# A four-layer hybrid decoder trunk: all instructions ordered with the timeline simulation instead of the core simulation

## The chip, the cores and the metric

The kernel runs on one core of one Trainium2 chip. The metric is the device time of one execution in microseconds (us), and the figure that counts is the median of several runs. Engine names in this text: PE (TensorE, matmuls), PEld (its weight loads), DVE (VectorE), ACT (ScalarE), POOL (GpSimd), SP (the queue that issues DMAs).

## The reference

Four layers work on x of 1024 tokens by 1024 channels in float32. Layer i has the token mixer i mod 3, so the order is convolution, S5, RWKV-7, convolution:

```python
for i in range(DEPTH):
    kind, j = i % N_MIXERS, i // N_MIXERS
    ...
    r = DN_ALPHA * x + y
    r = r + (p[i] @ ple_proj[i]) * jax.nn.sigmoid(r @ ple_gate[i])
    x = layer_norm(r, ln_g[i], ln_b[i])
```

Here y is the mixer's result. The convolution mixer is W_out(Bg * conv3(Cg * h) * silu(z)). The S5 mixer is a diagonal complex state-space scan in 64 groups of 16 channels, with a gated linear unit. The RWKV-7 mixer has 16 heads of 64 channels; each head keeps a 64x64 state that is updated token by token with a decay, a delta-rule term and an outer product:

```python
sa = jnp.einsum("bhvk,bhk->bhv", state, -kk_t)
state = (state * w_t[:, :, None, :] + sa[..., None] * (kk_t * a_t)[:, :, None, :]
         + v_t[..., None] * k_t[:, :, None, :])
out = jnp.einsum("bhvk,bhk->bhv", state, r_t)
```

## The kernel before, in words

Channels lie on the 128 partitions, in 8 blocks (`m`), and tokens on the free axis, in two halves of 512 (`h`). Every large product is `mm3` (L308 to L310): operand and weight are each split into a high and a low part, and for each of 8 slices of the inner dimension there are three matmuls of 128x512 (high by high, low by high, high by low), so 24 matmuls for one block and one half, summed in one PSUM bank. The weights come block by block through `wload` (L282 to L286): a DMA of 512 KB from SP's queue, an ACT cast that makes the high part `wh` (L285) and a DVE subtraction that makes the low part `wl` (L286). `wprep` keeps two blocks loaded ahead, from three buffers each.

The RWKV layer does its recurrence in chunks of 64 tokens. For each half it first computes z and v for all blocks, and then goes through the eight blocks in rounds. In a round, for block m:

- the key and the receptance products run (`k_mm` and the `mm3` inside `use_r`; their PSUM tile is `sp`), with the elementwise work on them in `use_k` and `use_r`;
- `prep` forms the chunk matrices (`s`, L1700) and lays their small diagonal blocks side by side with one DVE transpose (L1719, once per round);
- `tsolve` inverts the 16x16 diagonal blocks on DVE, and `join` builds the inverses of the 64x64 chunk matrices from them with 32x32 and 64x64 matmuls (L1780 to L1831);
- `seq` steps through 8 chunks: POOL scales the state (L1856), PE multiplies it (L1857), ACT copies the result (L1858), PE multiplies again (L1861), DVE updates the state (L1864). Then the output is normalised (POOL, L1892) and transposed on PE (L1899).

`join` and `seq` of block m are worked in during the round of block m+1. In the code that reads:

```python
for _ in prio(I.prep(m, h, R), PJ):
    pull(nxt_b)
if m > 0:
    for _ in prio(I.join(m - 1, h, Rs[m - 1]), PJ):
        pass
    inner.append(prio(I.seq(m - 1, h, Rs[m - 1], dVT, dST, dBV, dZ, dY), PS))
tsol.append(prio(I.tsolve(R), PT))
```

The order of the work has two makers. The code traces instructions in a program order, and generators (`pull`) mix background work into it by hand-set counts. That order gives each instruction its priority; `prio` raises the priority of `prep`, `join`, `seq` and `tsolve`. When the `TileContext` closes, a list scheduler goes through the whole trace on a simulated machine: each time an engine of the simulation can take an instruction, it gets the one of highest priority that is ready. What comes out is one fixed sequence of instructions per engine queue, SP's DMA issues among them, and with it the choice of buffers. On the chip each queue then runs in that sequence. A few orders are fixed by hand and hold in any simulation: `issue_after` and `run_of` queue runs of small matmuls behind each other, and `keep_in_program_order` pins the load of the exponential table before the rounds.

The function that opens the context, and that the diff touches:

## Time and profile before

| What | us |
|---|---|
| median of 3 runs | 2887.89 |
| lowest and highest of the runs | 2884.99, 2892.94 |
| the profiled execution, its own time | 2891.85 |
| its span in the profile | 2890.1 |
| PE busy in it | 2732.9 |

The profile is of one execution. Its own time is 1.75 us longer than the span that the trace covers. A busy PE is not PE at its peak: matmuls overlap each other and their weight loads. The granted clock (PEclk, or the column after the engines in a window) is given as a share of full speed. In a line of the chain of waits, "PE p L1861 <- ACT uv L1858: 24.4, 26, 5.4" means that PE stood 24.4 us in all, 26 times, at most 5.4 us, before the instruction of L1861 that writes `p`, until ACT's instruction of L1858 on `uv` was done.

### The profile page before, as it was taken

How to read it: one execution, taken by the hardware profiler on the slowest of the kernel's cores; microseconds unless marked ns; L12 is line 12 of the kernel's file. 1: busy time of each engine (PE TensorE's matmuls, PEld its weight loads, DVE VectorE, ACT ScalarE, POOL GpSimd, SP SyncE). 2: the span in 40 equal slices, each digit the busy share in tenths (PEclk: the TensorE clock that was granted, in tenths of full speed). 3: DMA queues.
4: the chain of work that ended last, by engine and by line, in shares of the span. 5: the costliest groups of instructions: out<-in, count | busy, mean ns of one | idle time of the engine just before them, and what ended most of it. 6: DMA issues, size and time to landing. Idle time of an engine off the chain costs nothing. (4 is left out here: it accounts for less than half of the span.)

```text
span 2890.1 us, 47194 instructions
## 1 busy us (share of the span) xinstructions
PE 2732.9 (95%) x18331; PEld 2164.9 (75%) x18331; DVE 1825.3 (63%) x3396; ACT 1122.2 (39%) x2163; POOL 652.3 (23%) x772
## 2 busy tenths in 40 slices
PE   8999999999999999999887899988899999999998
PEld 6887788778877887676666576766677778888887
DVE  6787855476757348877666587766657473333654
ACT  3333322242254224665455575555434231112322
POOL 1243413121107033102333211333342210000000
PEclk9999999999999999999988799998899999999999
DMA  5333322257873234462222254222334332112321
GB/s 165 97 95 95 95 77 66 88 170 210 224 245 110 88 99 131 155 192 94 78 73 82 77 185 134 85 69 81 102 103 137 104 88 58 52 44 66 117 66 38
DMA packets 449776, 313.10 MB, mean 108 GB/s; under 512 B 48360, under 2 KB 393744, under 8 KB 449552
## 3 DMA queue, kind: packets, MB, share of 16 engines
q1 hardware_dynamic: 449552, 310.08, 35.8%
q8 instruction: 144, 2.36, 0.3%
q14 instruction: 80, 0.66, 0.1%
HBM read 240.28 MB, written 69.21 MB: 107 GB/s over the span
## 5 line engine op out<-in xcount | busy, mean ns | idle before, releaser
L285 ACT CAST wh<-wraw 128x1024 fp32r<-128x1024 f32 x283 | 297.2, 1050 | 699.3 <-PE gp L309 186.5
L286 DVE TENSOR_TENSOR wl<-wraw,wh 128x1024 fp32r<-128x1024 f32 x283 | 369.7, 1306 | 314.9 <-ACT wh L285 309.3
L1856 POOL TENSOR_SCALAR sd<-state,pc 128x128 f32<-128x128 f32 x128 | 94.9, 744 | 214.1 <-DVE state L1864 213.6
L1864 DVE SCALAR_TENSOR_TENSOR state<-p,pc,sd 64x64 f32<-64x64 f32 x256 | 72.2, 282 | 73.6 <-PE p L1861 62.0
L621 POOL TENSOR_TENSOR ln_s<-ln_s,rp 128x512 f32<-128x512 f32 x42 | 61.0, 1452 | 208.1 <-DVE rp L617 208.1
L1861 PE MATMUL p<-uv,kbt 128*128 128x128 f32 x256 | 67.2, 348 | 26.1 <-ACT uv L1858 24.4
L1861 PEld LDWEIGHTS p<-uv,kbt 128*128 128x128 f32 x256 | 44.3, 210 | 57.6 <-ACT uv L1858 49.6
L1857 PE MATMUL p<-state,ra 128*128 128x128 f32 x256 | 64.2, 336 | 15.7 <-DVE state L1864 15.0
L308 PE MATMUL zp<-x_0h,wh 128*128 128x512 f32 x192 | 76.8, 400 | 0.0
L310 PE MATMUL gp<-r_0h,wl 128*128 128x512 f32 x192 | 76.8, 400 | 0.0
L310 PE MATMUL gp<-r_1h,wl 128*128 128x512 f32 x192 | 76.2, 397 | 0.5 <-DVE wl L286 0.5
L1858 ACT COPY uv<-p 64x128 f32<-64x128 f32 x128 | 33.3, 261 | 111.5 <-PE p L1857 109.9
L308 PE MATMUL gp<-r_1h,wh 128*128 128x512 f32 x192 | 76.4, 398 | 0.0
L309 PE MATMUL gp<-r_0l,wh 128*128 128x512 f32 x192 | 76.3, 397 | 0.0
L1857 PEld LDWEIGHTS p<-state,ra 128*128 128x128 f32 x256 | 44.2, 208 | 42.6 <-DVE state L1864 31.2
L308 PE MATMUL gp<-r_0h,wh 128*128 128x512 f32 x192 | 76.1, 396 | 0.0
L308 PE MATMUL zp<-x_1h,wh 128*128 128x512 f32 x192 | 76.0, 396 | 0.0
L310 PE MATMUL zp<-x_0h,wl 128*128 128x512 f32 x192 | 75.8, 395 | 0.0
L310 PE MATMUL zp<-x_1h,wl 128*128 128x512 f32 x192 | 75.7, 395 | 0.0
L309 PE MATMUL zp<-x_1l,wh 128*128 128x512 f32 x192 | 75.7, 394 | 0.0
L309 PE MATMUL zp<-x_0l,wh 128*128 128x512 f32 x192 | 75.7, 394 | 0.0
L636 POOL TENSOR_TENSOR rp<-r_0h,r_0l 128x512 f32<-128x512 f32 x24 | 38.5, 1630 | 164.1 <-PE op L309 164.0
(755 smaller groups left out, 8429.4 us busy)
## 6 DMA issues: line engine op xcount, KB each, us to landing
wraw<-in_conv_w_in_dram SPq DMA_DIRECT2D x80, 512.0 KB
wraw<-in_rwkv_w_rkvz_dram SPq DMA_DIRECT2D x64, 512.0 KB
wraw<-in_ple_gate_dram SPq DMA_DIRECT2D x56, 512.0 KB
wraw<-in_conv_w_out_dram SPq DMA_DIRECT2D x24, 512.0 KB
wraw<-in_ssm_w_in_dram SPq DMA_DIRECT2D x21, 512.0 KB
xt<-xd SPq DMA_DIRECT2D x32, 256.0 KB
wraw<-in_rwkv_w_out_dram SPq DMA_DIRECT2D x16, 512.0 KB
wraw<-in_ple_proj_dram SPq DMA_DIRECT2D x14, 512.0 KB
```

What stands on the lines that cost most here:

```text
L285: nc.scalar.copy(wh, raw)
L286: nc.vector.tensor_tensor(wl, raw, f32(wh[:]), ALU.subtract)
L308: nc.tensor.matmul(ps, lh, xh, start=(k == 0), stop=False)
L309: nc.tensor.matmul(ps, lh, xl, start=False, stop=False)
L310: nc.tensor.matmul(ps, ll, xh, start=False, stop=(k == kt - 1))
L621: nc.gpsimd.tensor_tensor(s, s, rs, ALU.add)
L636: (eng or nc.gpsimd).tensor_tensor(rs, f32(rh[:]), f32(rl[:]), ALU.add)
L1856: G.tensor_scalar(sd, st, R.pc[:, c:c + 1], None, ALU.mult)
L1857: nc.tensor.matmul(p1, R.ra[:, c, :], st, start=False, stop=False, skip_group_check=True)
L1858: SC.copy(uv[rb, :], p1[rb, :])
L1861: last = nc.tensor.matmul(p2[:, 0:P], R.kbt[c // 4][:, c % 4, :], uv, start=True, stop=True)
L1864: V.scalar_tensor_tensor(st[cs, cs], p2[cs, cs], R.pc[cs, c:c + 1], sd[cs, cs], ALU.mult, ALU.add)
```

## The change

One argument is added where the context is opened. The simulated machine on which the scheduler orders the instructions is then the library's timeline simulation instead of its core simulation. The computation, the tiles, the buffers and the dependencies that the code traces are the same.

```diff
-    with tile.TileContext(nc) as tc:
+    with tile.TileContext(nc, schedule_with_timeline_sim=True) as tc:
         body(tc, aps, out)
```

## Prediction

> **What bounds the kernel now.** I read the page first (busy shares and slices), then the windows by stage, then the chain of waits in the one stage that is not full. The page:
>
> ```profile
> span 2890.1 us, 47194 instructions
> PE 2732.9 (95%) x18331; PEld 2164.9 (75%) x18331; DVE 1825.3 (63%) x3396; ACT 1122.2 (39%) x2163; POOL 652.3 (23%) x772
> ...
> PE   8999999999999999999887899988899999999998
> ...
> PEclk9999999999999999999988799998899999999999
> ```
>
> TensorE is busy for 2732.9 of 2890.1 us, so it idles for 157 us; the slices put that idle time, and the low granted clock, mostly into slices 19 to 29. The windows by stage (time, then busy time and count of PE, PEld, DVE, ACT, POOL, then granted clock, DMA share, GB/s) sharpen this:
>
> ```profile
> 0.00:1120.00 1120.00, 1093.90 (x5167) 882.22 (x5168) 726.26 (x1238) 355.44 (x518) 303.27 (x359) 1.00 0.44 127
> 1120.00:1300.00 180.00, 169.13 (x733) 125.47 (x731) 153.19 (x230) 110.57 (x182) 29.84 (x36) 0.98 0.55 174
> 1300.00:1640.00 340.00, 288.22 (x4169) 218.13 (x4169) 233.81 (x579) 177.12 (x464) 102.16 (x139) 0.87 0.26 80
> 1640.00:1800.00 160.00, 145.20 (x743) 110.01 (x741) 113.67 (x196) 101.74 (x204) 24.57 (x25) 0.97 0.49 154
> 1800.00:2120.00 320.00, 282.06 (x4145) 216.32 (x4143) 212.63 (x547) 161.69 (x454) 104.35 (x134) 0.90 0.27 85
> 2330.00:2890.00 560.00, 548.82 (x2457) 448.29 (x2455) 253.81 (x426) 137.74 (x221) 22.62 (x30) 0.99 0.22 65
> ```
>
> Before 1120 us (conv and S5 layers) and after 2330 us (the last conv layer) PE is idle for 26 and 11 us of 1680 us. An order of instructions can give back next to nothing there; it can only lose. The two stretches 1300:1640 and 1800:2120 are the RWKV rounds (per block of 128 channels: key, receptance, `prep`, `tsolve`, `join`, and the recurrence `seq` of the block before). There PE idles for 52 + 38 = 90 us, and the granted clock is 0.87 and 0.90. So these 660 us are where the order decides.
>
> What bounds a round? One instruction marks each: the transpose of L1719, once per round.
>
> ```profile
> 1407.84 1.95 DVE L1719 STREAM_TRANSPOSE mi<-dg 128x1024 f32<-128x1024 f32 x1 [0.34 <-ACT dg L1713]
> 1452.48 1.95 DVE L1719 STREAM_TRANSPOSE mi<-dg 128x1024 f32<-128x1024 f32 x1 [0.34 <-ACT dg L1713]
> ...
> 2011.57 1.95 DVE L1719 STREAM_TRANSPOSE mi<-dg 128x1024 f32<-128x1024 f32 x1 [0.34 <-ACT dg L1713]
> 2054.86 1.95 DVE L1719 STREAM_TRANSPOSE mi<-dg 128x1024 f32<-128x1024 f32 x1 [0.50 <-ACT dg L1713]
> ```
>
> One round took 1452.48 - 1407.84 = 44.6 us, the other 2054.86 - 2011.57 = 43.3 us. Now the wide matmuls (tile sp: the key and receptance products, 128x512) in windows about as long as a round, and the same windows for all work:
>
> ```profile
> 1392.00:1434.00 42.00, 17.22 (x54) 9.36 (x52) 2.79 (x4) 1.24 (x2) 0.96 0.28 88
> ...
> 1519.00:1561.00 42.00, 1.95 (x8) 1.24 (x7) 2.79 (x4) 1.37 (x2) 0.76 0.35 110
> ...
> 2010.00:2050.00 40.00, 0.00 (x0) 0.00 (x0) 2.88 (x4) 0.00 (x0) 0.62 0.13 40
> ```
>
> Around the start of the first of these rounds, 42 us hold 54 wide matmuls among the small ones; the round that began at 2011.57 had none in its first 38 us, and was no shorter. So a round is not set by PE's load: it is a chain through PE, ACT, DVE and POOL of some 43 us, and the wide matmuls ride in its gaps for nothing. That cover is what the order of PE makes.
>
> **The change part by part.** It removes and adds no instruction of the computation, no tile and no buffer. It redraws the order on every queue (PE, ACT, DVE, POOL and the DMA issues of SP) by asking another simulated machine when each instruction is ready. Dependencies, priorities and the orders fixed by hand stay. I can't see the new order; I price it by what an order is worth in each stage.
>
> *Gain: PE instructions that stand too early.* The old order sent some PE instructions out before their input, and the in-order engine stood. From 1120 to 2330 us, PE's waits:
>
> ```profile
> PE p L1861 <- ACT uv L1858: 24.4, 26, 5.4
> PE otp L1899 <- POOL o L1892: 16.4, 14, 2.4
> PE p L1857 <- DVE state L1864: 15.0, 18, 2.2
> ...
> PE ut L1789 <- ACT zi L1786: 10.4, 9, 3.3
> ```
>
> That is 24.4 + 16.4 + 15.0 + 10.4 = 66.2 us in 67 waits, about 1 us each: a simulation that times ACT, DVE and POOL better would put another instruction first. At most 66 us come back; but the rounds are chains, and a matmul that fills such a gap helps only if it was not covered elsewhere. I take half: -33 us. Next behind each removed stall is the same chain's ACT or DVE step.
>
> *Loss: cover.* The pace of wide matmuls comes from a stretch that holds almost nothing else:
>
> ```profile
> 2600.00:2650.00 50.00, 50.00 (x217) 40.46 (x216) 16.98 (x22) 8.15 (x11) 2.85 (x4) 1.00 0.21 61
> ```
>
> 50 / 217 = 0.230 us each. One round's key and receptance products are 2 x 24 = 48 matmuls, 11.1 us. An order that issues them in one run, because their weights are ready, holds the chain up for as long, or leaves a later round bare. In the two stretches PE runs these:
>
> ```profile
> 1300.00:1640.00 340.00, 122.87 (x370) 68.99 (x370) 19.54 (x28) 8.85 (x14) 0.87 0.26 80
> 1800.00:2120.00 320.00, 85.92 (x255) 46.44 (x253) 16.94 (x24) 7.49 (x12) 0.90 0.27 85
> ```
>
> 370 + 255 = 625, or 144 us: that is the most that lost cover costs; the least is a gain, if the two or so rounds that are bare today were filled (2 x 11 = 22 us). The old order leaves about two of the sixteen rounds bare. For the new one I take four more, nearer to the old order than to the end: 4 x 11.1 = +44 us. The bare windows also show the clock at 0.76 and 0.62 against 0.96, which stretches the small matmuls. The bare round at 2011.57 was not longer for it; the other one, by its marks below, took 1577.49 - 1531.31 = 46.2 us. So the bounds are 0 and 46.2 - 44 = 2 us a round. I take 2: +8 us.
>
> ```profile
> 1531.31 1.94 DVE L1719 STREAM_TRANSPOSE mi<-dg 128x1024 f32<-128x1024 f32 x1 [0.39 <-ACT dg L1713]
> 1577.49 2.01 DVE L1719 STREAM_TRANSPOSE mi<-dg 128x1024 f32<-128x1024 f32 x1
> ```
>
> PE's longest wait from 1519 to 1561 us, in the chain of waits of that window:
>
> ```profile
> PE ut L1789 <- ACT zi L1786: 3.3, 1, 3.3
> ```
>
> [...]
>
> *The weights.* Each weight block is split by one ACT and one DVE instruction, and its slot's next load waits for the second:
>
> ```profile
> L285 ACT CAST wh<-wraw 128x1024 fp32r<-128x1024 f32 x283 | 297.2, 1050 | 699.3 <-PE gp L309 186.5 <-issue 121.5 <-PE op L309 96.7
> L286 DVE TENSOR_TENSOR wl<-wraw,wh 128x1024 fp32r<-128x1024 f32 x283 | 369.7, 1306 | 314.9 <-ACT wh L285 309.3 <-PE mu L676 2.7 <-PE kbtp L1465 0.5
> ```
> ```profile
> SPq L282 <- DVE wl L286: 1127.5, 209, 14.2
> ```
>
> Two blocks are kept ahead, and PE works on one block for 24 x 0.230 = 5.5 us and more; the pair takes 1.05 + 1.31 = 2.4 us, so it is hidden, and I cost it at 0. If it is put behind a run of side work, a block comes late by up to that pair: 2.4 us times 283 at the very most. SP stands up to 14.2 us on such a load, and a reload of `ga`, `cs` or `uv` placed behind it would keep a round waiting as long; no such wait is among PE's longest today, so 0 here too.
>
> *Sum:* -33 + 44 + 8 = +19 us on the profiled run. Its time is 2891.85 us, of which 2890.1 is the span, and 4.0 above the median of 2887.89; so the median becomes 2887.9 + 19 = 2907 us.
>
> **The rivals.**
> 1. *Faster: the waits go and no cover is lost.* For it: the stalls above are short and many, as from wrong durations, and 14 of them come from one POOL step. Against: a PE stall inside a chain of 43 us shortens the chain only where PE was its next step. -33 us gives 2855; with all 66 us, 2822.
> 2. *Slower in another place: the weight split comes late.* The conv layer with the S5 preparation in its background is where DVE is fullest (726 us of the first 1120). If one block in ten comes late by a pair, 28 x 2.4 = 67 us: 2955. It decides as soon as the side work ahead of a split is longer than the two blocks of lead, 2 x 5.5 = 11 us. Against: PE idles for 26 us in all there today.
> 3. *No change.* Rounds stay 43 us because the chain sets them, the rest is full of PE work either way, and the new order is in effect the old one: 2888. The change not doing what it says (the same order comes out) ends here too. Against: 47194 instructions are ordered anew, and 90 us of idle time are there to move.
>
> **How the numbers follow.** Two runs of this kernel differ by up to 0.3%, 8.7 us, so that is what a measurement can tell from no change. Forecast (cover lost, a little outweighing the waits) 0.38; rival 2, 0.12; together slower 0.50. Rival 1, faster, 0.37. Rival 3, same, 0.13. I lean to slower because the sides are unequal: 66 us of PE waits stand to be won, 144 us of cover and a split that is free today stand to be lost. The forecast's own range, with two to ten more bare rounds, is 2881 to 2985: 2 x 13 - 33 = -7 to 10 x 13 - 33 = +97, at 13 us a bare round. Eight times in ten: from 2835, most of the way into rival 1, to 2985, the forecast's upper end, which holds rival 2 as well.
>
> **What would show it.** Right: in the changed trace the wide matmuls come in longer runs, more windows of the rounds have an sp count near 0 and a clock under 0.8, the marks of L1719 lie further apart than 43 us or the stretch outside them has grown, and the four waits above have shrunk. Wrong: the marks lie closer with sp counts as now (rival 1), or PE's waits on wh and wl grow before 1120 us (rival 2). A changed time with the rounds as long as before, and PE as full elsewhere, would leave all of this without a cause.

## The result: 3114 us, 7.7% slower, and the profile after

| | before | after |
|---|---|---|
| median of the runs shown with the result | 2889.62 us (2884.99 to 2892.94) | 3113.53 us (3102.64 to 3116.76, 4 runs) |
| ratio after/before, 95% interval | | 1.077 (1.074 to 1.080) |
| span of the profiled run | 2890.1 us | 3113.2 us |

The forecast was 2907 us, eight times in ten between 2835 and 2985. The direction is right; the size is far outside the range. The page of the changed kernel:

```profile
span 3113.2 us, 47252 instructions
...
PE 2852.0 (92%) x18331; PEld 2290.5 (74%) x18331; DVE 1831.2 (59%) x3396; ACT 1119.5 (36%) x2165; POOL 653.4 (21%) x772
...
PE   8999999989989997888888888888897999999998
...
PEclk9999999989999998887776689778798999999999
```

TensorE executes the same 18331 matmuls, yet is busy 119 us longer (2852.0 - 2732.9), and idle 104 us longer (261 against 157). In the clock row five slices were under 9 before, the lowest at 7; now fifteen are, all but one in slices 16 to 31, and two are at 6. So two things have to be explained: more waiting, and the same instructions taking longer.

To place the 223 us I cut both traces at the same instructions: the first S5 product, the first S5 gate product, the first low-rank product of the RWKV layer (L1346), the first and the last L1719 of each half, and the last mean of L676, which ends the layer. The time of each stage, and what the change added:

| stage | before, us | after, us | added |
|---|---|---|---|
| first conv layer | 609.1 | 611.7 | +2.6 |
| S5 layer | 232.3 | 255.4 | +23.1 |
| S5 gate and output | 318.9 | 322.2 | +3.3 |
| z and v, first half | 149.2 | 203.3 | +54.1 |
| rounds, first half | 268.0 | 321.9 | +53.9 |
| z and v, second half | 211.7 | 250.0 | +38.3 |
| rounds, second half | 265.7 | 288.7 | +23.0 |
| end of RWKV, its output product | 261.6 | 280.6 | +19.0 |
| last conv layer and rest | 573.6 | 579.4 | +5.8 |

"z and v" is the stretch between the layer's start and its rounds, where the z and value products run. It adds 92 us, the rounds 77, and these four stages hold 169 of the 223. In the kernel before, the windows of these four (time, busy time and count of PE, PEld, DVE, ACT, POOL, then granted clock, DMA share, GB/s) are:

```profile
1160.30:1309.50 149.20, 144.66 (x678) 105.10 (x677) 119.59 (x191) 95.80 (x164) 12.27 (x10) 1.00 0.55 177
1309.50:1577.50 268.00, 225.74 (x3235) 172.54 (x3230) 187.08 (x475) 139.54 (x375) 84.39 (x115) 0.89 0.26 81
1577.50:1789.10 211.60, 189.53 (x1551) 141.50 (x1551) 144.19 (x263) 127.35 (x272) 39.16 (x46) 0.91 0.42 129
1789.10:2054.90 265.80, 231.06 (x3241) 179.39 (x3243) 181.87 (x474) 136.69 (x371) 83.55 (x109) 0.88 0.26 80
```

The same four in the changed kernel:

```profile
1189.30:1392.60 203.30, 165.06 (x676) 119.47 (x677) 120.56 (x190) 97.16 (x164) 10.60 (x12) 0.87 0.42 134
1392.60:1714.50 321.90, 268.34 (x3224) 219.71 (x3221) 187.97 (x477) 142.42 (x380) 81.37 (x112) 0.74 0.21 65
1714.50:1964.50 250.00, 215.91 (x1582) 166.09 (x1581) 139.99 (x264) 126.89 (x270) 38.91 (x48) 0.82 0.36 114
1964.50:2253.20 288.70, 246.71 (x3238) 199.14 (x3238) 183.83 (x476) 134.05 (x369) 83.83 (x109) 0.78 0.23 71
```

The first pair behind each window's length is PE. Its counts are equal within 2%, and its busy time grows from 791.0 to 896.0 us (+105) while the clock falls from 0.88–1.00 to 0.74–0.87. PE's idle time (window less busy) grows from 103.6 to 167.9 us (+64). DVE, ACT and POOL do the same work in the same busy time. So no work is added anywhere: TensorE stands more, and runs at a lower clock. Busy time times granted clock, summed over the four rows, is 721 us before and 712 after, so the lower clock accounts for about all of the longer busy time.

The longest waits of PE in the whole changed kernel, to set beside the four rows that the prediction wanted shrunk (the 66.2 us of those rows are also their sum over the whole kernel before):

```profile
PE p L1857 <- DVE state L1864: 41.1, 48, 2.1
PE p L1861 <- ACT uv L1858: 26.8, 50, 1.9
PE pw L1378 <- ACT w L1376: 21.0, 11, 5.3
PE wps L1724 <- DVE sca L1705: 13.2, 9, 5.7
...
PE otp L1899 <- POOL o L1892: 7.2, 2, 7.0
PE ut L1789 <- ACT zi L1786: 7.0, 2, 4.1
```

The four add up to 82.1 us in 102 waits, against 66.2 in 67. They moved, and they did not shrink.

**The rounds.** The wide products (tile sp) between two marks of L1719 in the kernel before:

```profile
1452.48:1496.81 44.33, 17.88 (x48) 9.61 (x48) 2.10 (x3) 1.25 (x2) 0.86 0.23 73
...
1531.31:1577.49 46.18, 4.75 (x12) 2.35 (x12) 2.79 (x4) 0.00 (x0) 0.74 0.30 100
...
2011.57:2054.86 43.29, 0.00 (x0) 0.00 (x0) 2.19 (x3) 0.00 (x0) 0.65 0.21 71
```

and in the changed one:

```profile
1461.25:1515.90 54.65, 15.48 (x48) 11.26 (x48) 2.79 (x5) 1.27 (x2) 0.77 0.20 60
...
1665.25:1714.47 49.22, 7.19 (x16) 4.63 (x17) 1.35 (x2) 0.00 (x0) 0.62 0.14 45
...
2030.58:2078.30 47.72, 14.25 (x48) 9.78 (x47) 2.78 (x4) 1.27 (x2) 0.80 0.22 69
...
2127.31:2172.95 45.64, 12.69 (x48) 8.60 (x47) 2.78 (x4) 1.27 (x2) 0.78 0.23 72
...
2215.52:2253.16 37.64, 0.00 (x0) 0.00 (x0) 1.35 (x2) 0.00 (x0) 0.73 0.27 88
```

The first two rounds of each half are shorter in both kernels. From the third on, a round took 40 to 46 us before, with 39 to 60 wide matmuls, with 12 or with none (the one with 24 took 34.5): they rode for nothing. After, the rounds with 48 or 49 take 45.6 to 54.7 us, and the one without any takes 37.6. Within the second half the difference is 8.0 to 11.4 us, about the 48 x 0.230 = 11.0 us that 48 take by themselves. That the wide matmuls now pay for themselves is argued from this one bare round, which is also 5.7 us shorter than the bare one before; in the first half the round with only 16 still takes 49.2 us. The number of rounds without any did not change (one in each kernel). What changed is how the 48 stand in PE's queue. I counted runs of wide products with no other matmul between them, from the first matmul of L1826 (in `join`) to the end, so with the second half's z and v: 976 in 213 runs before, 936 in 77 runs after; and 335 against 735 of them stood in runs of 18 or more.

**The z and v stretch.** The order there is a regular pattern: 18 wide matmuls, the narrow low-part products pw and pa (L1379), 6 wide, the products of the high part (L1378), 18 wide, and so on. The timeline of one such block in the changed kernel (start, time, instruction, and in brackets the idle time before it and what ended it):

```profile
1241.48 0.80 PE L308 MATMUL sp<-xs3h,wh 128*128 128x512 f32 x1 [0.57 <-DVE sg L1368]
1241.55 0.28 DVE L1377 TENSOR_TENSOR w<-rwkv_a,w 128x128 fp32r<-128x128 f32 x1
...
1248.25 0.39 PE L1379 MATMUL pw<-lhl,w 128*128 128x512 f32 x1
...
1248.74 0.69 ACT L1381 ACTIVATE sw<-pw,vec 128x512 f32<-128x512 f32 x1 [7.68 <-PE pw L1379]
...
1251.97 1.04 ACT L285 CAST wh<-wraw 128x1024 fp32r<-128x1024 f32 x1
...
1255.24 0.29 ACT L1376 CAST w<-rwkv_w 128x128 fp32r<-128x128 f32 x1
...
1255.58 0.80 PE L1378 MATMUL pw<-lhl,w 128*128 128x512 f32 x1 [5.32 <-ACT w L1376]
```

The weights of pw and pa are ready at 1241.8 (L1377 runs 0.28 us from 1241.55). PE starts their low part at 1248.25, behind 18 wide matmuls. ACT stands 7.68 us for it, then works off what queued behind, L1376 for the next block among it, and PE stands 5.32 us for that. The engines take turns where they overlapped: ACT's waits on pw at L1381 are 57.6 us in the first half's stretch, 13.7 before. The matmuls at 1241.48 and 1255.58 take 0.80 us, where those at 1248 take 0.39. The granted clock was 0.50 from 1240.2 to 1246.9 us, 1.00 from 1247.0 to 1253.7, and 0.50 again when PE resumed:

```profile
1253.80:1264.00 10.20, 6.69 (x15) 4.81 (x16) 6.88 (x12) 3.78 (x8) 0.00 (x0) 0.50 0.25 78
```

### The profile page after: what moved, and what is told of

Read it like the earlier page. It is cut to its first block, busy times and chain, and to the rows that moved or that the text cites. A ratio compares the mean times of both kernels' runs of the same rounds, so it can differ in the third digit from the quotient of the medians.

```text
span 3113.2 us, 47252 instructions
## 1 busy us (share of the span) xinstructions
PE 2852.0 (92%) x18331; PEld 2290.5 (74%) x18331; DVE 1831.2 (59%) x3396; ACT 1119.5 (36%) x2165; POOL 653.4 (21%) x772
## 5 line engine op out<-in xcount | busy, mean ns | idle before, releaser
L286 DVE TENSOR_TENSOR wl<-wraw,wh 128x1024 fp32r<-128x1024 f32 x283 | 362.4, 1281 | 345.5 <-ACT wh L285 339.8
L1857 PE MATMUL p<-state,ra 128*128 128x128 f32 x256 | 74.4, 380 | 42.2 <-DVE state L1864 41.1
L1857 PEld LDWEIGHTS p<-state,ra 128*128 128x128 f32 x256 | 49.7, 237 | 64.6 <-DVE state L1864 55.3
L309 PE MATMUL gp<-r_1l,wh 128*128 128x512 f32 x192 | 75.6, 394 | 0.0
```

What stands on the lines that cost most here:

```text
L286: nc.vector.tensor_tensor(wl, raw, f32(wh[:]), ALU.subtract)
L309: nc.tensor.matmul(ps, lh, xl, start=False, stop=False)
L1857: nc.tensor.matmul(p1, R.ra[:, c, :], st, start=False, stop=False, skip_group_check=True)
```

## The experiments

**Theories.** A: the timeline simulation lets each simulated engine take a number of instructions ahead, and PE so many that it has always accepted a block of wide matmuls before a narrow step becomes ready, so narrow steps are queued behind blocks. B: the durations and latencies of that simulation make the order, whatever the depth. C: the same look-ahead as in A, but on ACT, VectorE and GpSimd.

### How deep the simulated queues are

Each of these kernels is the changed one with one setting of the simulation more ahead of the kernel's build: how many instructions it lets an engine take ahead (P for PE, O for the others). The changed kernel sets neither; I took its own for 35 and 12.

```diff
+    ... = {SP: O, Activation: O, DVE: O, Pool: O, PE: P}
```

d_pe1 (P = 1, O = 12):

> The changed kernel, but the timeline simulation that makes the order is told that PE's queue holds 1 instruction ahead instead of 35; the queues of the other engines stay at 12. Same computation, only the order differs. Theory A (the new order is bad because the simulated PE takes some 35 wide matmuls ahead, so that a small matmul that becomes ready is put behind them): most of the 224 us come back, 2860 to 2930 us, the marks of L1719 are 40 to 45 us apart again, and in the z phase PE's waits at L1378 fall from 23 us to under 6 us. Theory B (the durations and latencies of the timeline simulation make the order, whatever the depth): 3060 to 3130 us. Theory C (the look-ahead of ACT, DVE and POOL does it): 3060 us or more as well.

d_o1 (P = 35, O = 1):

> The changed kernel with PE's simulated queue left at 35 and those of ACT, DVE, POOL and SP at 1 instead of 12. Theory A (PE's look-ahead): stays at 3080 to 3130 us. Theory B (durations): the same. Theory C (the look-ahead of ACT, DVE and POOL puts side work ahead of steps that PE waits for): 2900 to 2980 us.

d_pe1_o1 (P = 1, O = 1):

> The changed kernel with all simulated queues at 1. Theory A: as with PE alone at 1, within 20 us of it. Theory C: better than PE alone at 1 by 50 us or more. Theory B: 3060 us or more. If A and C both hold a part, it is the fastest of the four, 2840 to 2900 us.

d_pe4 (P = 4, O = 12):

> The changed kernel with PE's simulated queue at 4, the others at 12. Theory A: a small matmul then stands behind at most some 4 wide ones (0.9 us), so the time lies near that of depth 1, 10 to 40 us above it. Theory B: no dependence on the depth, 3060 us or more.

d_pe8 (P = 8, O = 12):

> The changed kernel with the simulated PE queue 8 instructions deep instead of 35 (other engines 12 as in the change). Theory A: the loss grows with the depth, so between depth 4 (2920) and depth 35 (3113): 2925 to 3010. Rival B (depth 4 was a lucky order, each depth gives an order of its own with no trend): anywhere from 2900 to 3250, and not between its neighbours 4 and 16.

d_pe16 (P = 16, O = 12):

> The changed kernel with the simulated PE queue 16 instructions deep. Theory A: between depth 8 and depth 35, 2980 to 3090. Rival B (no trend): outside the times of its neighbours 8 and 35 by more than 20 us.

d_pe2 (P = 2, O = 12):

> The changed kernel with the simulated PE queue 2 instructions deep: 196 runs of wide matmuls from the first round to the last, 5.0 in a mean run, against 4.6 before and 5.9 at depth 4. Theory A (the time follows the mean run, and depth 1 falls out of the row for a reason of its own: with one instruction in flight the simulated PE is slower than everything else): 2880 to 2925. Rival B (shallow queues are worse again, in steps): between 2920 and 3244, above 2950.

| kernel | time, us | ratio to before (95%) | runs of wide products, mean run |
|---|---|---|---|
| before | 2885 to 2892 | 1 | 213, 4.6 |
| d_pe2 | 2911.37 | 1.007 (1.006 to 1.009) | 196, 5.0 |
| d_pe4 | 2920.05 | 1.011 (1.009 to 1.013) | 162, 5.9 |
| d_pe8 | 2953.79 | 1.023 (1.020 to 1.027) | 128, 7.4 |
| d_pe16 | 3002.77 | 1.040 (1.036 to 1.043) | 104, 9.0 |
| after (35) | 3113.53 | 1.077 (1.074 to 1.080) | 77, 12.2 |
| d_o1 (35, others 1) | 3110.07 | 1.078 (1.075 to 1.081) | 77, 12.2 |
| d_pe1 | 3244.06 | 1.124 (1.122 to 1.126) | 322, 3.2 |
| d_pe1_o1 | 3250.68 | 1.125 (1.123 to 1.128) | 322, 3.2 |

With 35 written out, d_o1 has the runs of wide products of the changed kernel (77, 12.2 in the mean) and its time within 4 us, so the changed kernel stands at 35 in the series. The depths are settings of the simulation; how far the chip's engines take instructions ahead, no run here tells.

C falls: the others' depth changes nothing measurable (3110 against 3114; at P = 1, 3251 with O = 1 against 3244 with O = 12). B falls: depth 4 alone takes 193 of the 224 us back. From 2 to 35 the time follows the mean run of wide matmuls, step by step, as A says. The rounds alone are 0.5, 6, 23, 54 and 77 us longer than before at depths 2, 4, 8, 16 and 35. But A's forecast for depth 1 failed wholly: 2860 to 2930 expected, 3244 measured, with the shortest runs of all; and so did the one for depth 4, which was set 10 to 40 us above depth 1 and came out 324 us below it. There all rounds but the first of each half take 55 to 67 us. In its first half's rounds PE is idle for 382.50 - 293.02 = 89.5 us against 42.3 before:

```profile
1416.50:1799.00 382.50, 293.02 (x3406) 210.86 (x3405) 191.83 (x501) 151.09 (x409) 86.55 (x124) 0.75 0.21 61
```

Its largest wait there, L1826 on VectorE's tt, adds up to 14.2 us in six waits; in the whole kernel before it is 0.8 us, once. A simulated PE with one instruction in flight may look so slow that the other engines' work is put off; that is an argument, and no run shows it. In these kernels short runs were needed, and did not suffice.

### One place in the z loop

z_pin is the changed kernel with the wide matmuls of product m queued behind the last low-part product of block m-3, from the fourth product on:

```diff
+            elif m >= 3:
+                with S.tc.issue_after(lows[m - 3].ins):
+                    ps = z_mm(m, h)
```

> The changed kernel with one pin in its order: in the second loop over the z products (from the fourth product on), the 24 wide matmuls of product m are queued on PE behind the last low-part product (L1379) of block m-3, so that the low-part products no longer stand behind 18 of the 24. Theory A (the look-ahead of the simulated PE queue puts wide matmuls ahead of narrow ones whose inputs come a little later, and engines then run in lockstep): the two z and v stretches, 92 us longer than before, come down to 0 to 40 longer; the rounds keep their +77; total 3030 to 3080. Rival B (what carries the loss there is the order of ACT and VectorE, or the clock, not this place in PE's queue): the stretches keep 70 or more of the 92, total 3090 to 3120.

z_late is the kernel before, with the opposite pin, which makes its low-part products stand where the change has them:

```diff
+            if m >= 3:
+                for i in lows[m - 3]:
+                    S.tc.add_manual_dep(i.ins, S.mm18.ins.name, ...)
```

> The kernel before with the suspected fault put in: in the z loop the low-part products (L1379) of block m-3 are queued on PE behind the 18th wide matmul of product m, as they stand in the changed kernel; all else as the core simulation orders it. Theory A: the z and v stretches grow by 30 to 90 us, total 2920 to 2980. Rival B: no more than 15 us, total 2880 to 2905, since the core simulation sees the dependency and can place the side work of ACT and VectorE around it.

z_pin took 3080.25 us (1.066, 1.063 to 1.069), its z and v stretches 38.5 + 27.5 = 66 us longer than before: 26 of the 92 came back, where A had wanted 52 or more. z_late took 2919.24 us (1.010, 1.007 to 1.013), its stretches 22.8 + 13.4 = 36 us longer. In z_late the wait that the timeline showed comes up out of nearly nothing:

```profile
PE pw L1380 <- ACT w L1378: 19.9, 7, 6.5
```

(line numbers are two higher there; before, the same wait is 2.7 us in 2). So the fault is real and it costs these stretches 26 to 36 us, put in or taken out; in z_late the second half's rounds came out 11.5 us shorter, which hides a part of it in the total. It is about a third of what the stretches lost, and not the whole as I had thought. With PE's whole order of before (x_pe, in the next part) they are 16.1 + 7.0 = 23 us longer, so 69 of the 92 lie in PE's order; at which other places in it is not shown.

### Whose order carries the loss

These kernels are built twice. The first build, with the core simulation, gives the order of before. The second uses the timeline simulation, with each instruction of the chosen engines pinned behind the one that preceded it on its engine in the first. The pins ask for issue order alone and make no engine wait for another.

```diff
+            for k in order:
+                i = traced[k]
+                if i.engine in engines:
+                    if i.engine in last:
+                        tc.add_manual_dep(i, last[i.engine].name, NoSync, ...)
+                    last[i.engine] = i
...
+    _, _, seq = build()
+    nc, arrays, _ = build(seq, (PE,), schedule_with_timeline_sim=True)
```

Only the list of engines differs.

x_pe (PE):

> PE executes its instructions in exactly the order that it has in the kernel before; the orders of ACT, VectorE, GpSimd and SyncE are made by the timeline simulation, as in the change. Theory A (the loss is in PE's order alone: wide matmuls in blocks of 24 between the narrow steps, 77 runs of them in the stretch from the first round to the last against 213 before): the loss of 225 us goes, 2870 to 2920. Rival B (the order of the other engines carries half or more): 3000 or more.

x_rest (ACT, VectorE, GpSimd):

> ACT, VectorE and GpSimd execute their instructions in exactly the order of the kernel before; PE's order (and SyncE's) is made by the timeline simulation with its queue of 35. It has the wide matmuls of that stretch in 71 runs. Theory A: the loss stays, 3060 to 3160 (a PE queue that is fitted to a foreign order of the other engines can be worse than either). Rival B: 2890 to 3000.

x_pesp (PE, SyncE):

> PE and SyncE in exactly their orders of before, ACT, VectorE and GpSimd by the timeline simulation. Theory SP (the 77 us left with PE fixed are late or early transfers in SyncE's queue): 2885 to 2915. Theory AV (they are the order of ACT and VectorE, the weight split among it): 2945 to 2975.

x_sp (SyncE):

> SyncE alone in its order of before, all other engines by the timeline simulation. Theory SP: 60 to 80 us come back, 3030 to 3060, the S5 stage among them. Theory AV: 3090 to 3120.

x_pead (PE, ACT, VectorE):

> PE, ACT and VectorE in exactly their orders of before, SyncE and GpSimd by the timeline simulation. Theory SP: 2945 to 2975. Theory AV: 2885 to 2915.

x_pea (PE, ACT):

> PE and ACT in exactly their orders of before, VectorE, GpSimd and SyncE by the timeline simulation. With PE alone fixed, PE waits longer than before for results of VectorE above all (state L1864 25.4 us against 15.0, tt L1814 11.8 against 0.8, kb L1444 8.9 against 1.9, w L1377 6.9 against 0.6). Theory V (small operations of the scan stand behind wide ones in VectorE's queue): 2940 to 2970. Theory S (ACT's order, the weight split that it starts among it): 2885 to 2910.

x_ped (PE, VectorE):

> PE and VectorE in exactly their orders of before, ACT, GpSimd and SyncE by the timeline simulation. Theory V: 2885 to 2910. Theory S: 2940 to 2970.

| engines in their order of before | time, us | ratio to before (95%) |
|---|---|---|
| none (after) | 3113.53 | 1.077 (1.074 to 1.080) |
| SyncE | 3151.22 | 1.091 (1.089 to 1.093) |
| ACT, VectorE, GpSimd | 3175.77 | 1.099 (1.097 to 1.100) |
| PE | 2968.42 | 1.027 (1.025 to 1.029) |
| PE, SyncE | 2986.41 | 1.034 (1.032 to 1.036) |
| PE, ACT | 2947.02 | 1.019 (1.017 to 1.022) |
| PE, VectorE | 2920.05 | 1.010 (1.008 to 1.013) |
| PE, ACT, VectorE | 2887.66 | 0.999 (0.997 to 1.000) |

PE's order alone takes back 3113.5 - 2968.4 = 145 of the 222 us (the kernel before ran at 2891.9 beside it), so PE's order carries two thirds. Theory A had wanted nearly all, 2870 to 2920, and fell short: the remaining 77 us are ACT's and VectorE's, since with their orders fixed as well nothing is left (2887.66 beside 2890.97). Beside x_pe, VectorE's order takes back 48 us, ACT's 21, both together 81. Theory V holds for the larger part: x_pea is in its range, x_ped 10 us above it, so some of the rest is ACT's. Depth 2 alone had taken back 202 of 224 us; there the orders of ACT and VectorE are made anew beside PE's. In x_pe PE waits longer for VectorE than in the kernel before, as in these rows (there 15.0, 0.8, 1.9 and 0.6 us):

```profile
PE p L1857 <- DVE state L1864: 25.4, 24, 2.5
...
PE p L1826 <- DVE tt L1814: 11.8, 5, 3.9
...
PE kbtp L1465 <- DVE kb L1444: 8.9, 5, 4.2
PE pw L1379 <- DVE w L1377: 6.9, 4, 3.3
```

The other engines' old order without PE's makes it worse (3176 against 3114, above A's range too), and SyncE's old order, alone or beside PE's, too: x_sp and x_pesp lie above the forecasts of both theories. Here an order was good only beside the orders that it was made with. SyncE's and GpSimd's new orders cost nothing (x_pead); theory SP falls. Why SyncE's old order costs 38 us with the others new (x_sp) was not tried further; against the changed kernel its S5 stage is 15 us longer, z and v of the second half and the end of RWKV 21 each, and the second half's rounds are 19 shorter.

### A version that might beat both

d_pe2 was faster than before in the second half's rounds (-6.0) and after them (-4.3). x_hyb keeps all engines in their orders of before for the first 9221 instructions of PE (to the end of the first half's rounds), and leaves the rest to the timeline simulation with P = 2:

```diff
+    while n < 9221:
+        n += seq[cut] in pe
+        cut += 1
...
+    nc, arrays, _, _ = build(seq[:cut], (PE, Activation, DVE, Pool, SP), schedule_with_timeline_sim=True)
```

> All engines in their orders of before up to the end of the first half's rounds (9221 of PE's instructions), from there the timeline simulation with a PE queue of 2. If the stages are independent, the sum of the stages as d_pe2 measured them against before: -1.0 (z and v of the second half) -6.0 (its rounds) -4.3 (tail) +1.7 +1.0 = -9, that is 2876 to 2886 beside a kernel before of 2887. If the early part's order was what the later stages profited from: 2887 to 2900.

It took 2890.40 us beside 2890.97, ratio 1.000 (0.999 to 1.001): no gain, as its second range had it. By its profile the second half's rounds are 1.0 us shorter, the stage after them 3.3 us shorter, the last conv layer 5.0 us longer; the first conv layer, whose order is that of before, is 4.1 us shorter, so differences of this size show nothing. No kernel here is faster than the one before by more than 0.3%, and the 23 runs of that one beside x_hyb span 0.6%.

## Why the prediction was wrong in size

**The order outside the rounds was priced at nothing.** The prediction looked at the stretches before 1120 us and after 2330 us, wrote that an order "can only lose" there, and put nothing for that loss into its sum (rival 2 had a price for a late weight split alone). Two stretches between (1120 to 1300, 1640 to 1800 us) were quoted and not priced at all, and the one from 2120 to 2330 us was not shown. This is the step that failed. They were near full (PE 94% and 91% busy), and I took fullness for safety. It was what the old order had achieved: a side chain PE, ACT, VectorE, PE ran through it, hidden. z and v lost 92 us, the S5 layer 23, the end of RWKV 19, and 12 elsewhere: 146 of the 223. The direction came out right, then, mostly by a loss that the sum did not hold, and its +19 us were the small difference of a gain that did not come and a loss that was larger.

**Cover.** The sentence gave two ways in which a run of wide matmuls hurts: it "holds the chain up for as long, or leaves a later round bare". I priced the second, four more bare rounds. The first is what the depth series speaks for: there are as many rounds without wide matmuls as before, one (of the two that I had counted as bare, the one at 1531 held 12), and the rounds grow with the mean run, by 0.5 us at 5.0 and by 77 at 12.2. These 77 us stand against +44 for cover and +8 for the clock. "144 us: that is the most" was a bound for the rounds alone; it was not passed there, and could not hold for the stages that it left out.

**The waits.** Half of 66.2 us was to come back. They are 82.1 us now. L1857 behind VectorE's state went from 15.0 to 41.1, L1899 from 16.4 to 7.2, L1789 from 10.4 to 7.0. That "a simulation that times ACT, DVE and POOL better would put another instruction first" had nothing in the profile to rest on: a wait shows that an order is imperfect, and not that another simulation mends it.

**The clock.** I took 2 us a round from one comparison of two bare rounds. That small matmuls were longer there, the trace of before shows: those of L1831 took 317 ns each in the two windows that I took for bare (clock 0.76 and 0.62) and 225 in the other (0.96). In the four stages PE's matmuls, the same before and after, took 105 us longer, beside 64 us of added idle time; so the slower matmuls are the larger part. The clock did not follow the idle time. In the first half's rounds PE idles for 16% of the time before and 17% after, and the clock goes from 0.89 to 0.74. The depth series pulls the two apart. The rounds of d_pe2:

```profile
1332.80:1607.40 274.60, 233.68 (x3221) 184.35 (x3220) 192.49 (x478) 141.31 (x377) 82.65 (x113) 0.85 0.25 78
1818.10:2077.80 259.70, 223.12 (x3228) 177.36 (x3228) 185.50 (x474) 136.47 (x370) 83.08 (x108) 0.88 0.26 82
```

and of d_pe8:

```profile
1338.30:1625.80 287.50, 233.89 (x3199) 186.37 (x3198) 187.13 (x474) 140.34 (x378) 78.77 (x112) 0.83 0.24 74
1842.60:2111.90 269.30, 223.04 (x3199) 177.74 (x3198) 182.97 (x468) 133.26 (x365) 83.68 (x107) 0.87 0.25 78
```

From depth 2 to 8 PE's busy time stays (456.8 and 456.9 us) and its idle time grows from 77.5 to 99.9. From 8 to 35 the idle time does not grow (95.5 at 35), and the clock falls to 0.74 and 0.78 and the busy time grows by 58 us. So from 8 to 35 all of the 54 us that the rounds grew by are slower matmuls: the longer blocks came with a lower clock, and not with more waiting.

**The weights.** Priced at 0, and right: the first conv layer, where VectorE is fullest, took 2.6 us more, and no wait of PE on a weight is among its longest. SyncE's longest wait for a split grew from 14.2 to 18.9 us without harm that shows.

```profile
SPq L282 <- DVE wl L286: 1145.3, 208, 18.9
```

Rival 2 is out by that. Rivals 1 and 3 are out by the time. The one sign I had given for "longer runs of wide matmuls" was the right one to look for, and could not be seen beforehand: the depth that makes them is a setting of the simulation and stands in no view of the kernel before.

## What to carry to other kernels

A stage that is 95% full under the present order says what that order achieved, and not what any order would: before an edit that redraws the order, find the narrow chains that run hidden through the full stages, and price each as if it stood behind one whole block of wide work. In a new order look first at the mean run of the wide instructions on the bounding engine, and in a timeline at what stands queued ahead of a narrow one whose input is ready; then at the granted clock, which cost more here than the idle time did (105 against 64 us). Here a simulated queue that ran further ahead made longer runs (5.0 in the mean at depth 2, 12.2 at 35), and the time rose with its depth at each step from 2 to 35, from 2911 to 3114 us; depth 1 was worse than all, at 3244.

## What the runs showed of the hardware

In one stretch the granted clock fell before there was a long wait. The windows of the changed kernel at the start of a round, in steps of 3 us:

```profile
1407.00:1410.00 3.00, 3.00 (x19) 2.55 (x18) 0.00 (x0) 0.31 (x1) 0.00 (x0) 1.00 0.57 171
1410.00:1413.00 3.00, 2.63 (x21) 1.67 (x20) 1.89 (x3) 1.71 (x3) 0.00 (x0) 1.00 0.13 49
1413.00:1416.00 3.00, 2.03 (x16) 1.89 (x16) 1.29 (x4) 1.93 (x6) 0.00 (x0) 0.70 0.72 212
1416.00:1419.00 3.00, 0.47 (x4) 0.18 (x1) 1.29 (x3) 1.91 (x4) 0.00 (x0) 0.50 0.64 226
1419.00:1422.00 3.00, 2.46 (x74) 2.34 (x77) 2.98 (x6) 2.91 (x8) 2.09 (x3) 0.50 0.00 0
1422.00:1425.00 3.00, 3.00 (x53) 1.90 (x43) 2.90 (x6) 1.73 (x4) 0.67 (x2) 0.59 0.03 5
1425.00:1428.00 3.00, 3.00 (x15) 2.46 (x14) 0.72 (x3) 0.00 (x0) 0.00 (x0) 1.00 0.00 0
```

PE's waits in this stretch:

```profile
PE wps L1724 <- DVE sca L1705: 3.1, 1, 3.1
PE s L1700 <- DVE scr L1707: 1.0, 2, 0.8
PE s L1700 <- DVE kp L1478: 0.4, 1, 0.4
```

From 1413 to 1416 us the clock is 0.70 on average, so it went to half within that window, while PE ran small matmuls (L1700, 64x128) with no wait of over 0.8 us; the 3.1 us wait began at 1416.5. In steps of 0.5 us the fall lies between 1414.0 and 1414.5 (0.70, then 0.50), and the clock is back at 1.00 from 1424.5 on, about 10 us later. So here the fall came ahead of the longest wait of the stretch. In the kernel before the clock went to half at 1905 us behind 3.4 us in which PE was busy throughout by the profile; the third row has the wide matmuls of the first window, one of its 71:

```profile
1901.60:1905.00 3.40, 3.40 (x71) 2.87 (x68) 3.17 (x11) 2.62 (x12) 0.31 (x1) 1.00 0.24 63
1905.00:1908.40 3.40, 3.40 (x45) 3.09 (x43) 1.97 (x8) 1.30 (x9) 0.19 (x1) 0.50 0.01 2
...
1901.60:1905.00 3.40, 0.51 (x1) 0.19 (x1) 0.75 (x1) 0.00 (x0) 1.00 0.24 63
```

The ends of matmuls are modelled in the profile, so this busy time is not full use of PE. In both stretches small matmuls ran ahead of the fall: L1700 alone from 1411.0 to 1414.2 us, and the 70 others of those 71. What brings a fall about, and what use of PE keeps the clock up, no run here tells.
